# A rotary-embedding kernel: the last store in two pieces, and another row for the shared work

## Chip, cores and metric

One core of a Trainium2 chip. The metric is device time in microseconds (us) of one execution. The time is some 1.75 us above the span of the profile of the same execution, so differences can be compared between the two.

## The reference

`x` is (16, 512, 1024) float32: 16 heads of 64 in each row. Every head is rotated:

```python
x = x.reshape(batch, seq, num_heads, head_dim)
x1, x2 = (x[..., :half_dim].copy(), x[..., half_dim:].copy())
rotated = np.concatenate([x1 * cos - x2 * sin, x1 * sin + x2 * cos], axis=-1)
```

33.6 MB are read and 33.6 MB written.

## The kernel before

The work is cut into eight tiles of 128 partitions x 8 rows of 1024 values (4096 KB each), which live in five slots of one buffer `xt` and are computed in place. In each tile, row 1 goes through VectorE, TensorE and ScalarE ("own row"); one row gets its cosine product from VectorE, its sine product from GpSimd, and is added by TensorE ("shared row"); the other six rows go in pairs: GpSimd makes the sine product, VectorE the cosine product and the sum. All loads and stores of `x` are issued by SyncE on one queue.

```python
ROW_OWN, ROW_PE = 0, 3
PAIRS = ((1, 2), (4, 5), (6, 7))
...
def stores(t):
    if t == 1:
        store(0, 0, 2 * KK)      # tiles 0 and 1 together
    elif t > 1:
        store(t)                 # one tile, 8 rows, 32 KB in each partition
    if t == 2:
        load(5)
        load(6, 0, 2 * KK)
...
for t in range(NT):
    first, second, third = PAIRS
    b1 = sin_rows(t, first[0], 2)            # GpSimd
    cos_product(own_ps, t, ROW_OWN)          # VectorE
    ...                                      # own row
    p1 = pair_product(t, first[0])           # VectorE
    b3 = sin_rows(t, ROW_PE, 1)
    b2 = sin_rows(t, second[0], 2)
    pair_sum(*p1, b1)
    p2 = pair_product(t, second[0])
    cos_product(own_ps, t, ROW_PE)
    for ps, b in zip(parts(own_ps), parts(b3)):
        pe_add(ps, b)                        # TensorE
    nc.scalar.copy(out=rows(t, ROW_PE), in_=own_ps)
    b1 = sin_rows(t, third[0], 2)
    ...
    pair_sum(*p2, b2)
    p1 = pair_product(t, third[0])
    pair_sum(*p1, b1)
    stores(t)
```

Tiles and rows are counted from 0 in the code and from 1 in the text. As the first two tiles share a store, there are seven stores; "the sixth store" is that of the last tile but one and is issued near 132 us (the seventh tile's store), the seventh store is the last.

## Time and profile before

| | before |
|---|---|
| time, three runs | 163.22, 163.30, 163.31 us |
| profiled execution: time, span | 163.58, 161.8 us |
| VectorE busy | 137.8 us (85%) |
| the DMA queue of all loads and stores | 97.0% of 16 engines' span |
| last store: issued, landed | 149.9, 161.0 us |

The prediction shows the lines behind these numbers and how they are read. In the lines PE is TensorE (PEld its weight loads), DVE VectorE, ACT ScalarE, POOL GpSimd and SPq SyncE's queue of instructions; q1 is the DMA queue of the loads and stores of `x`, q14 that of instruction fetches. Two things to know ahead: a DMA is spread over 16 engines and has landed when the slowest of them has; and the DMA share and GB/s in windows count each packet whole in the window where it starts, so short windows can show more than the engines can do.

### The profile page before, as it was taken

How to read it: one execution, taken by the hardware profiler on the slowest of the kernel's cores; microseconds unless marked ns; L12 is line 12 of the kernel's file. 1: busy time of each engine (PE TensorE's matmuls, PEld its weight loads, DVE VectorE, ACT ScalarE, POOL GpSimd, SP SyncE). 2: the span in 40 equal slices, each digit the busy share in tenths (PEclk: the TensorE clock that was granted, in tenths of full speed). 3: DMA queues.
4: the chain of work that ended last, by engine and by line, in shares of the span. 5: the costliest groups of instructions: out<-in, count | busy, mean ns of one | idle time of the engine just before them, and what ended most of it. 6: DMA issues, size and time to landing. Idle time of an engine off the chain costs nothing.

```text
span 161.8 us, 432 instructions
## 1 busy us (share of the span) xinstructions
PE 64.5 (40%) x72; PEld 20.5 (13%) x72; DVE 137.8 (85%) x77; ACT 18.5 (11%) x20; POOL 126.9 (78%) x38
## 2 busy tenths in 40 slices
PE   2272671444518180818153542626090906262000
PEld 0121120202011110202020201111020202020000
DVE  1149899999999999999999999999999999999000
ACT  3010202020201010020202020202002020202000
POOL 1095999999499999999999699973999999940000
PEclk9999999995555555555855576556755585769555
DMA  5999999699699799799999999898999999996996
GB/s 171 407 410 470 405 502 518 292 486 518 275 486 535 308 470 518 340 429 397 429 464 397 478 437 502 389 405 381 437 462 397 437 462 397 446 454 275 389 389 259
DMA packets 2113, 67.25 MB, mean 416 GB/s; under 512 B 256, under 2 KB 256, under 8 KB 320
## 3 DMA queue, kind: packets, MB, share of 16 engines
q1 hardware_dynamic: 2064, 67.18, 97.0%
q10 hardware_dynamic: 48, 0.07, 0.1%
q14 instruction: 1, 0.01, 0.0%
HBM read 33.69 MB, written 33.55 MB: 416 GB/s over the span
## 4 chain that ended last, share of the span: by engine, by line
DVE 35%; DMA 33%; POOL 13%; issue 9%; PE 2%; ACT 1%; DVEq 0%; POOLq 0%; SPq 0%
DMA xt<-in_x_dram 17%; DMA out_dram<-xt 17%; DVE pd L152 15%; DVE xt L201 14%; POOL b L175 13%; DVE own_ps L152 2%; PE own_ps L186 2%; DVE xt L158 2%; ACT xt L193 1%; DVE small L119 0%; DVEq L201 0%; POOLq L175 0%; SPq L77 0%; SPq L81 0%
## 5 line engine op out<-in xcount | busy, mean ns | idle before, releaser
L175 POOL TENSOR_TENSOR b<-xt,sns 128x2048 f32<-128x2048 f32 (+1 forms) x32 | 126.2, 3987 | 15.9 <-DMA xt<-in_x_dram 15.9
L201 DVE TENSOR_TENSOR xt<-pd,b 128x2048 f32<-128x2048 f32 x24 | 54.9, 2289 | 1.6
L152 DVE TENSOR_TENSOR pd<-xt,cos_t 128x2048 f32<-128x2048 f32 x24 | 55.0, 2294 | 0.5
L186 PE MATMUL own_ps<-xt,ident 128*128 128x512 f32 x32 | 29.7, 1081 | 42.7 <-DVE xt L158 22.2
L186 PE MATMUL own_ps<-b,ident 128*128 128x512 f32 x32 | 29.7, 1085 | 33.2 <-DVE own_ps L152 30.8
L152 DVE TENSOR_TENSOR own_ps<-xt,cos_t 128x1024 f32<-128x1024 f32 x16 | 19.6, 1222 | 3.4 <-PE cos_t L122 3.0
L186 PEld LDWEIGHTS own_ps<-xt,ident 128*128 128x128 f32 x32 | 9.4, 323 | 62.4 <-issue 62.4
L186 PEld LDWEIGHTS own_ps<-b,ident 128*128 128x128 f32 x32 | 9.4, 324 | 53.5 <-issue 37.7
L193 ACT COPY xt<-own_ps 128x1024 f32<-128x1024 f32 x8 | 8.1, 1012 | 64.4 <-PE own_ps L186 64.4
L228 ACT COPY xt<-own_ps 128x1024 f32<-128x1024 f32 x8 | 8.1, 1012 | 55.1 <-PE own_ps L186 55.1
L158 DVE TENSOR_TENSOR xt<-xt,small 128x1024 f32<-128x1024 f32 x8 | 9.8, 1220 | 0.2
L123 DVE TENSOR_SCALAR sns<-small 128x256 f32<-128x256 f32 x1 | 0.4, 424 | 4.7 <-PE small L116 4.7
L116 PE MATMUL small<-sin_sb,spread 32*128 32x256 f32 x4 | 2.2, 662 | 2.8 <-DMA sin_sb<-in_sin_dram 2.8
L122 PE MATMUL cos_t<-cos_sb,spread 32*128 32x512 f32 x2 | 2.1, 1136 | 2.1 <-DMA cos_sb<-in_cos_dram 2.1
L116 PEld LDWEIGHTS small<-sin_sb,spread 32*128 32x128 f32 x4 | 1.2, 320 | 4.8 <-issue 4.8
L99 PE MATMUL own_ps<-zero 128*128 128x512 bf16 x2 | 1.0, 621 | 1.2 <-DVE zero L96 1.2
L124 ACT ACT_TABLE_LOAD x1 | 1.3, 1283 | 1.2 <-PEq L252 1.2
L96 DVE MEMSET zero<- 128x256 uint32 x1 | 0.3, 272 | 0.9 <-PEq L252 0.9
L124 ACT COPY sns<-small 128x256 f32<-128x256 f32 x1 | 0.4, 372 | 4.3 <-DVE sns L123 4.3
L127 ACT ACTIVATE sns<-small 128x256 f32<-128x256 f32 x1 | 0.4, 383 | 4.2 <-PE small L116 4.2
L122 PEld LDWEIGHTS cos_t<-cos_sb,spread 32*128 32x128 f32 x2 | 0.5, 308 | 2.8 <-DMA cos_sb<-in_cos_dram 2.8
L119 DVE COPY small<-sns 128x64 f32<-128x64 f32 x2 | 0.4, 224 | 0.4 <-ACT sns L124 0.4
(9 smaller groups left out, 1.6 us busy)
## 6 DMA issues: line engine op xcount, KB each, us to landing
out_dram<-xt SPq DMA_DIRECT2D x6, 4096.0 KB, 22.4
xt<-in_x_dram SPq DMA_DIRECT2D x3, 4096.0 KB, 21.8
xt<-in_x_dram SPq DMA_DIRECT2D x1, 2560.0 KB, 12.6
xt<-in_x_dram SPq DMA_DIRECT2D x1, 1536.0 KB, 7.2
sin_sb<-in_sin_dram ACTq DMA_DIRECT2D x1, 64.0 KB, 4.2
cos_sb<-in_cos_dram SPq DMA_DIRECT2D x1, 64.0 KB, 7.1
xt<-in_x_dram SPq DMA_DIRECT2D x2, 34.9
out_dram<-xt SPq DMA_DIRECT2D x1, 26.7
```

Source lines behind the costliest of these rows:

```text
L99: nc.tensor.matmul(out=ps, lhsT=zero[:, :P], rhs=zero, start=True, stop=True)
L116: nc.tensor.matmul(out=sin_t, lhsT=spread, rhs=part, start=True, stop=True)
L119: nc.vector.tensor_copy(out=own_t[:, u], in_=sns[:, u * KK + ROW_OWN].rearrange("p a j -> p (a j)"))
L122: nc.tensor.matmul(out=cos_t, lhsT=spread, rhs=cos_sb, start=True, stop=True)
L124: nc.scalar.copy(out=sns[:, :KK, 1, :], in_=sin_k)
L152: nc.vector.tensor_tensor(out=o, in0=i, in1=cb, op=ALU.mult)
L158: nc.vector.tensor_tensor(out=heads(r), in0=heads(r), in1=s, op=ALU.mult)
L175: nc.gpsimd.tensor_tensor(out=o, in0=i, in1=sb, op=ALU.mult)
L186: nc.tensor.matmul(out=ps, lhsT=ident, rhs=other, start=False, stop=True, skip_group_check=True)
L193: nc.scalar.copy(out=r0, in_=own_ps)
L201: nc.vector.tensor_tensor(out=r, in0=ps, in1=b, op=ALU.add)
L228: nc.scalar.copy(out=rows(t, ROW_PE), in_=own_ps)
```

## The change

Its intent is to start the last store earlier. With the shared row moved to the end, the first five rows of a tile are complete after the second of its three pair sums, so five eighths of the last tile can be stored while VectorE still works on the last pair.

```diff
-ROW_OWN, ROW_PE = 0, 3
+ROW_OWN, ROW_PE = 0, 7
-PAIRS = ((1, 2), (4, 5), (6, 7))
+PAIRS = ((1, 2), (3, 4), (5, 6))
 FIRST = 3
+LAST_OUT = 5
@@ def stores(t):
     if t == 1:
         store(0, 0, 2 * KK)
+    elif t == NT - 1:
+        store(t, 0, LAST_OUT)
+        store(t, LAST_OUT, KK)
     elif t > 1:
         store(t)
```

## The prediction

> **What bounds the kernel now.** I read the page first (busy shares, then the line of 40 slices for the DMA engines), then the chain of waits, then the last 30 us by windows, and last the time from issue to landing of each of the last stores.
>
> The page's shares and its DMA rows:
>
> ```profile
> PE 64.5 (40%) x72; PEld 20.5 (13%) x72; DVE 137.8 (85%) x77; ACT 18.5 (11%) x20; POOL 126.9 (78%) x38
> DMA  5999999699699799799999999898999999996996
> q1 hardware_dynamic: 2064, 67.18, 97.0%
> DVE 35%; DMA 33%; POOL 13%; issue 9%; PE 2%; ACT 1%; DVEq 0%; POOLq 0%; SPq 0%
> ```
>
> The fullest resource is not VectorE (85%) but the one DMA queue that carries all loads and stores (97% of 16 engines' span): 67.18 MB have to pass and they pass at a nearly constant rate. The chain of waits names VectorE most (35%), but it is the chain of the instructions that happen to end last. Whether VectorE or the queue sets the end has to be read from the last stage. Windows over it (columns: stretch and its length, then PE, PEld, DVE, ACT and POOL busy with instruction counts, granted clock, DMA share, GB/s):
>
> ```profile
> 115.00:132.50 17.50, 7.44 (x8) 2.34 (x8) 17.19 (x11) 2.02 (x2) 17.50 (x6) 0.61 1.00 431
> 132.50:148.15 15.65, 7.29 (x8) 2.34 (x8) 15.34 (x9) 2.02 (x2) 10.84 (x3) 0.67 1.01 436
> 148.15:150.20 2.05, 0.00 (x0) 0.00 (x0) 1.65 (x1) 0.00 (x0) 0.00 (x0) 0.86 0.08 32
> 150.20:161.80 11.60, 0.00 (x0) 0.00 (x0) 0.00 (x0) 0.00 (x0) 0.00 (x0) 0.50 0.84 362
> ```
>
> Until 148 us the DMA engines are full although VectorE is busy as well: the store queue has a backlog. At about 148 us it runs dry while VectorE is still at the last pair of the last tile, so for a moment VectorE does set the end. Then one whole store of 4096 KB runs by itself. The issues of the last three stores in the timeline (start, length), and under them their times from issue to landing, in the same order:
>
> ```profile
> 115.11 0.33 SPq L81 DMA_DIRECT2D out_dram<-xt  x1
> 132.49 0.33 SPq L81 DMA_DIRECT2D out_dram<-xt  x1
> 149.87 0.33 SPq L81 DMA_DIRECT2D out_dram<-xt  x1
> ...
> out_dram<-xt SPq DMA_DIRECT2D x1, 4096.0 KB, 25.7
> out_dram<-xt SPq DMA_DIRECT2D x1, 4096.0 KB, 17.9
> out_dram<-xt SPq DMA_DIRECT2D x1, 4096.0 KB, 11.1
> ```
>
> Sums: they land at 115.11 + 25.7 = 140.8, at 132.49 + 17.9 = 150.4 and at 149.87 + 11.1 = 161.0 us. The store before these (issued at 97.74, 33.4 us to landing) lands at 131.1. So inside the backlog one store lands every 9.6 us ((150.39 - 131.14) / 2 = 9.63), however early it was issued; the last one comes 10.6 us after its predecessor. The difference, 0.95 us, is all that the dry queue costs at the landing, and it is the number on which the prediction rests. After the landing 0.8 us are left to the end of the span.
>
> It is much less than the 2.05 us of nearly idle DMA in the third window. The finer windows show why:
>
> ```profile
> 148.20:148.40 0.20, 0.00 (x0) 0.00 (x0) 0.20 (x1) 0.00 (x0) 0.00 (x0) 1.00 0.38 164
> 148.80:149.00 0.20, 0.00 (x0) 0.00 (x0) 0.20 (x1) 0.00 (x0) 0.00 (x0) 1.00 0.39 164
> 149.00:150.50 1.50, 0.00 (x0) 0.00 (x0) 0.80 (x1) 0.00 (x0) 0.00 (x0) 0.71 0.00 0
> 150.50:150.80 0.30, 0.00 (x0) 0.00 (x0) 0.00 (x0) 0.00 (x0) 0.00 (x0) 0.50 3.30 1420
> ```
>
> 1420 GB/s cannot be a rate; a window counts each packet whole, where it starts. 164 GB/s x 0.2 us is 32.8 KB, one packet of one engine: so one engine starts its last packet of the sixth store at 148.2 to 148.4 and another at 148.8 to 149.0. A packet of 32,768 B takes 1.22 us (431 GB/s over 16 engines at share 1.00 is 26.9 GB/s each). The last engine is therefore busy until about 150.1, and its first packet of the last store starts after 150.5: it stood still for some 0.5 to 0.7 us, while the average engine stood still for about 1.5 us. The landing records of the trace, one for each engine, agree: the sixth store lands on 15 engines by 149.87 and on the last at 150.44, and the same 0.57 us lag is there in the stores before. A store has landed when its slowest engine has, so the slowest engine's gap counts.
>
> **What the Trainium skill says.** "DMA: Bandwidth & Descriptors", section "Queues, rings and completion order": each engine takes the descriptors of its ring in order, the engines of one transfer finish independently, and only the full count of 16 means landed. The trace agrees: even spacing of 9.6 us in the backlog, and the lagging engine. The same page, "Anatomy of one DMA": a DMA has a fixed part of about 2.0 us (fitted on the GpSimd path), and most of it is completion latency. Here the lone last store takes 11.1 us for 4.19 MB; at the 436 GB/s of the window that is 9.6 us of moving and 1.5 us fixed, of which a full queue hides the front but not the receipt at the end. "Latency and other measured facts" on that page gives about 600 ns to the first byte on the path that SyncE uses; the trace shows 149.87 to about 150.6, a bit more. The table "Measured" under "Bandwidth" gives 78% of the peak for a transfer of 1 MB alone; I do not apply that to pieces of 2.5 and 1.5 MB, as they are queued behind each other here.
>
> **The change part by part.**
>
> *The rows.* The shared row becomes the eighth and the pairs become rows 2-3, 4-5, 6-7. The built program keeps the same number and order of instructions on PE, VectorE, ScalarE and GpSimd, with the same shapes: 24 pair products of 2.29 us, 24 pair sums of 2.29 us, 32 GpSimd products, 32 + 32 matmuls. Only offsets move. For the first tile the load is split after row 3, and both orders need just rows 1-3 for the first GpSimd product and the second part for all others, so no wait moves. Cost 0. What it buys is that the first five rows of a tile are finished by the first two pair sums and the own row.
>
> *The early piece.* The timeline of the last tile:
>
> ```profile
> 138.79 1.01 ACT L193 COPY xt<-own_ps 128x1024 f32<-128x1024 f32 x1 [8.35 <-PE own_ps L186]
> 142.79 2.28 DVE L201 TENSOR_TENSOR xt<-pd,b 128x2048 f32<-128x2048 f32 x1
> 146.65 1.01 ACT L228 COPY xt<-own_ps 128x1024 f32<-128x1024 f32 x1 [6.84 <-PE own_ps L186]
> 147.50 2.29 DVE L201 TENSOR_TENSOR xt<-pd,b 128x2048 f32<-128x2048 f32 x1
> ```
>
> Row 1 is in place at 139.8, the second pair sum ends at 145.1, the shared row at 147.7, the third pair sum at 149.8. In the built program the store of five rows waits for the second pair sum and the own-row copy of the last tile and for nothing later; the store of three rows waits for the last sum and copy. So the five rows are issued at about 145.15 instead of 149.87, 4.7 us earlier. But the queue still holds the sixth store until 148 to 150. With some 0.8 us from issue to first packet the piece stands ready at 146, before even the fastest engine is free. The 4.7 us shrink to the gap.
>
> *The late piece.* It is issued at 149.87 as the whole store was, and can start at 150.6. Five eighths of 9.6 us is 6.0 us, so the slowest engine reaches the three rows at about 150.1 + 6.0 = 156, the fastest near 154.5. They are there 4 us too early, so the queue stays full to the end.
>
> *What it adds.* One more issue on SyncE (0.33 us, hidden) and packets of 20 KB and 12 KB in place of 32 KB. In the load of 20 KB rows at the start the engines moved 419 GB/s at share 0.98 (window 7.9 to 14.2), 26.7 GB/s each against 26.9: 0.8% of 9.7 us, 0.08 us. The receipt at the end stays as it is.
>
> *Sum.* Slowest engine: 150.4 + 9.63 + 0.08 = 160.1 instead of 161.0 from the rounded landings; with the records to the hundredth (150.44, and eight pairs of a 20 KB and a 12 KB packet at 0.766 and 0.460 us, 9.81) it is 160.25 instead of 160.96. So 0.7 to 0.9 us less; I take 0.8. 163.3 - 0.8 = 162.5 us, 0.5% faster.
>
> **The rivals.** (a) The full gap is won: if the average engine counted, 1.5 us or even the 2.05 us of the window, 161.8 to 161.2 us. For it speaks the empty window; against it that the lag of one engine persists from store to store. It would come true if the lag is a matter of chance in this execution. The record of an 8 KB instruction fetch of 0.32 us at 82 us, and the lag rising from 0.30 us before it to 0.57 us after, suggest part of it is regular. (b) Nothing is won: the early piece waits for the whole tile after all, or the two smaller transfers pay a second receipt in sequence. Then 163.3, or with 1 us more 164.3. The built waits speak against the first, the even spacing of queued stores against the second. (c) VectorE becomes the bound of the end: it does for the last three rows only if the queue is dry before 150.6, and it has 6 us of five rows left then. (d) A gain of 3.7 us, since just three eighths of the store remain after the last sum: 149.87 + 1.5 + 3.6 = 155. The backlog forbids it.
>
> **Range and chances.** The main doubt is which engine counts: gains from 0.3 us (slower small packets, lag a bit larger) to 1.5 us (no lag). I take 161.9 to 163.1. Two per cent is 3.3 us, more than the whole DMA gap, so within 2% is nearly sure.
>
> **What would show it.** In the profile after: an issue of 2560 KB near 145 and one of 1536 KB near 150; no empty DMA window at 148 to 150.5; the last landing near 160.2, some 9.7 to 9.8 us after that of the sixth store, with the engines now ending unevenly; unchanged groups for VectorE and GpSimd. A sixth store that lands elsewhere than at 150.4, or a last landing before 159.5 or after 160.8, would make it wrong.

## The result, and the profile after

Ratios are the mean time of one kernel's runs over that of the other's of the same rounds, so not quite the ratio of the medians that are quoted. The change was measured four times, the first time as the result proper, then as after_again, after_third and after_fourth.

| measurement | changed, median (range) | before, median (range) | ratio, 95% interval |
|---|---|---|---|
| result | 163.05 (162.51 to 163.45) | 163.32 (163.22 to 163.51) | 0.9981 (0.996 to 1.0002) |
| after_again | 162.71 (162.36 to 163.04) | 163.43 (163.20 to 163.85) | 0.9954 (0.9939 to 0.997) |
| after_third | 163.23 (162.95 to 163.60) | 163.44 (163.28 to 163.58) | 0.9988 (0.9976 to 1.000) |
| after_fourth | 163.32 (162.84 to 163.81) | 163.45 (163.24 to 164.22) | 0.9988 (0.9963 to 1.0012) |

The mean of the four ratios is 0.9978: 0.36 us of 163.4. The result's 163.05 us lies inside the predicted range, near its upper end. The mean gain is less than half of the 0.8 us forecast; only after_again comes near it (0.75 us), and in the other three measurements the interval reaches 1. In the result proper and in after_third the changed kernel also spreads more (0.94 us against 0.29, 0.65 against 0.30); in the other two the kernel before, with more runs, spreads as much (0.65 and 0.98 us).

In the profile of the changed kernel each step stands where the prediction put it. Its page, busy shares and chain of waits:

```profile
PE 64.5 (40%) x72; PEld 20.6 (13%) x72; DVE 137.8 (86%) x77; ACT 18.5 (11%) x20; POOL 126.9 (79%) x38
q1 hardware_dynamic: 2208, 67.18, 97.5%
DVE 67%; issue 16%; DMA 4%; POOL 3%; PE 2%; ACT 1%; DVEq 0%; POOLq 0%
```

No engine's work has changed. The chain of waits now says VectorE 67% and DMA 4%, which read alone would mislead: it starts at the last instruction of an engine, and the backlog in the DMA queue isn't an instruction. The windows over the end (columns as in the prediction):

```profile
132.50:148.15 15.65, 7.13 (x8) 2.35 (x8) 15.34 (x9) 2.02 (x2) 10.77 (x3) 0.68 1.01 436
148.15:150.20 2.05, 0.00 (x0) 0.00 (x0) 1.66 (x1) 0.00 (x0) 0.00 (x0) 0.79 0.84 362
150.20:161.80 11.60, 0.00 (x0) 0.00 (x0) 0.00 (x0) 0.00 (x0) 0.00 (x0) 0.50 0.71 303
```

The window that was nearly dry (share 0.08, 32 GB/s) now holds 0.84 and 362 GB/s. And the issues of the last stores in the timeline (start, length), with the time from issue to landing of each below, in the same order:

```profile
132.50 0.33 SPq L82 DMA_DIRECT2D out_dram<-xt  x1
145.16 0.33 SPq L82 DMA_DIRECT2D out_dram<-xt  x1
149.89 0.33 SPq L82 DMA_DIRECT2D out_dram<-xt  x1
...
out_dram<-xt SPq DMA_DIRECT2D x1, 4096.0 KB, 17.9
out_dram<-xt SPq DMA_DIRECT2D x1, 2560.0 KB, 11.3
out_dram<-xt SPq DMA_DIRECT2D x1, 1536.0 KB, 10.2
```

The sixth store lands at 150.4, the five rows at 145.16 + 11.3 = 156.5, the three rows at 149.89 + 10.2 = 160.1 us; before it was 161.0. The span is 161.0 against 161.8, and this execution took 162.75 us. So the pair of profiles shows the predicted 0.8 us. That is luck in part: the profile of the kernel before is of an execution of 163.58 us, slower than all six of its timed runs of the result, and that of the changed kernel is of one faster than its median. The other executions mostly did not gain as much, and what sets them apart is what the experiments had to find.

### The profile page after: what moved, and what is told of

Its sections match the earlier page's. It is cut to its first block, busy times and chain, and to the rows that moved or that the text cites. A ratio compares the mean times of both kernels' runs of the same rounds, so it can differ in the third digit from the quotient of the medians.

```text
span 161.0 us, 434 instructions
## 1 busy us (share of the span) xinstructions
PE 64.5 (40%) x72; PEld 20.6 (13%) x72; DVE 137.8 (86%) x77; ACT 18.5 (11%) x20; POOL 126.9 (79%) x38
## 4 chain that ended last, share of the span: by engine, by line
DVE 67%; issue 16%; DMA 4%; POOL 3%; PE 2%; ACT 1%; DVEq 0%; POOLq 0%
DVE pd L153 31%; DVE xt L202 25%; DVE own_ps L153 6%; DVE xt L159 5%; DMA xt<-in_x_dram 4%; POOL b L176 3%; PE own_ps L187 2%; ACT xt L194 1%; DVEq L202 0%; DVE small L120 0%; DVEq L159 0%; POOLq L176 0%
## 6 DMA issues: line engine op xcount, KB each, us to landing
out_dram<-xt SPq DMA_DIRECT2D x1, 2560.0 KB, 11.3
out_dram<-xt SPq DMA_DIRECT2D x1, 1536.0 KB, 10.2
```

## The experiments

Theory 1: the changed kernel ends when the slowest DMA engine has worked off its backlog, and how far that engine lags differs from execution to execution; the kernel before lets nearly every engine run dry and starts its last store level. Rivals: small pieces cost a varying extra; the moved rows cost something; the first measurement was chance; the sum on VectorE sets the end.

### Repeats, the rows alone, and other pieces

**after_again**: the changed kernel unaltered.

> The changed kernel, unaltered, once more. Theory 1 (lag): the changed kernel's end is the slowest DMA engine's backlog, which differs from execution to execution, while the kernel before lets every engine run dry at about 150 us and starts its last store level; so the runs spread again over 0.6 us or more (162.5 to 163.5), median near 163.0, and in the profile the span follows the landing of the sixth store on its slowest engine: last landing = that landing + 9.7 us. Theory 2 (pieces): the end costs a varying extra for two small transfers; then the distance from the sixth store's landing to the last landing varies and is over 9.9 us in a slow profile. Theory 3 (chance): the first measurement was off, now the median is 162.5 with a spread under 0.3 us.

**rows_only**: the changed kernel without the split store.

```diff
-    elif t == NT - 1:
-        store(t, 0, LAST_OUT)
-        store(t, LAST_OUT, KK)
```

> New rows and pairs, but the last tile stored whole as before. Theory 1: as the kernel before, 163.3 us within 0.15, spread under 0.35 us, last store's 16 engines landing within 0.25 us of each other. Theory 4 (the moved rows cost something that the pieces win back): 163.7 to 164.0. If the wide spread comes with the rows, it shows here.

**old_rows_six_two**: old rows and pairs, pieces of six and two rows.

```diff
-ROW_OWN, ROW_PE = 0, 7
-PAIRS = ((1, 2), (3, 4), (5, 6))
+ROW_OWN, ROW_PE = 0, 3
+PAIRS = ((1, 2), (4, 5), (6, 7))
-LAST_OUT = 5
+LAST_OUT = 6
```

> Old rows and pairs, the last tile stored in six and two rows: the six are complete when the fourth row's copy ends at about 147.7 us, so their store is issued near 147.75 and its packets are ready near 148.5, when the fastest engines have just run dry. Theory 1: as the changed kernel, 163.0 with a wide spread (0.6 us or more), because the slow engine decides and it still has work until 150; the rows are not needed. If the 4.7 us of earlier issue mattered in themselves it would lie at 163.3. Theory 2: pieces of 24 KB and 8 KB cost as much as those of 20 and 12.

**before_again**: the kernel before, unaltered.

> The kernel before, unaltered, as a null: ratio 1.000 within 0.0005, spread 0.3 us. Theory 1: its sixth store's slowest landing differs from that of the first profile by some tenths of a us, yet its last landing stays at 161.0 within 0.1 and its engines land within 0.25 us of each other. Theory 3: no difference of the sixth store's landing between profiles.

Measured on one chip: after_again 0.9954; rows_only 163.42 us, 0.9996 (0.9981 to 1.0011); old_rows_six_two 162.85 us, 0.996 (0.9946 to 0.9974); before_again 163.47 us, 0.9999 (0.9983 to 1.0014). The rows alone are worth nothing, and with the old rows a split of six and two gives what the change gives. So the moved rows were not needed. The spreads were not as clear-cut as expected: 0.68 us for after_again, 0.50 for old_rows_six_two, 0.66 and 0.53 for rows_only and before_again, whose VectorE began its work earlier or later by some tenths (their last store was issued at 149.68 and 149.75, against 149.87 before).

The profiles settle the mechanism. The sixth and the last store of after_again, issues and landings:

```profile
132.09 0.33 SPq L82 DMA_DIRECT2D out_dram<-xt  x1
149.47 0.33 SPq L82 DMA_DIRECT2D out_dram<-xt  x1
...
out_dram<-xt SPq DMA_DIRECT2D x1, 4096.0 KB, 18.6
out_dram<-xt SPq DMA_DIRECT2D x1, 1536.0 KB, 10.9
```

and of before_again:

```profile
132.37 0.33 SPq L81 DMA_DIRECT2D out_dram<-xt  x1
149.75 0.33 SPq L81 DMA_DIRECT2D out_dram<-xt  x1
...
out_dram<-xt SPq DMA_DIRECT2D x1, 4096.0 KB, 17.7
out_dram<-xt SPq DMA_DIRECT2D x1, 4096.0 KB, 11.1
```

In after_again everything on VectorE is 0.4 us earlier than in the first profile of the change, yet the sixth store takes 18.6 us in place of 17.9 and the end is at 149.47 + 10.9 = 160.4 in place of 160.1. In before_again the sixth store lands at 150.1, 0.3 us earlier than in the first profile, and the last again 11.1 us after its issue: the kernel before follows VectorE, the changed one the queue.

The landing records of each profile (one for each of the 16 engines) give the lag itself. "Lag" is the slowest engine's landing of the sixth store less the median engine's; the last columns are the time from the sixth store's landing to the last landing, and the spread of the 16 engines at the last landing.

| profile | lag | sixth to last landing | spread at the end |
|---|---|---|---|
| before | 1.17 us | 10.52 us | 0.17 us |
| before_again | 0.80 | 10.78 | 0.15 |
| rows_only | 0.66 | 10.85 | 0.15 |
| after | 1.16 | 9.72 | 1.46 |
| after_again | 1.43 | 9.72 | 1.78 |
| old_rows_six_two | 1.48 | 9.74 | 1.68 |
| after_third | 1.72 | 9.71 | 2.01 |
| after_fourth | 1.92 | 9.72 | 2.32 |

With a split store the last landing comes 9.71 to 9.74 us after the sixth, whatever the pieces, so the pieces cost nothing that varies; that rival falls. The lag is carried unchanged to the end. With a whole store the engines end level, and the lag shows in nothing but the middle column.

In this table the split kernels lag more than the others (1.16 us and up, against 1.17 and less). A rival would be that the change itself makes the lag. The lag stands already at the landing near 111 us (1.16 us in before, 1.14 in after), long before the split store is issued at 145 us, and further profiles cross over: at the sixth store the lag was 2.05 us in before_pad64 and 1.88 in before_more, with whole stores, and 0.43 in after_extra and 0.62 in one_engine, with split ones (all described below).

**after_third** and **after_fourth**: the changed kernel again, on two other chips.

> The changed kernel a third time. Theory 1 (a varying lag of the slowest engine on top of a steady 9.73 us): ratio 0.995 to 0.998, spread 0.6 us or more, and in the profile last landing = the seventh tile's slowest landing + 9.7 us. If the first measurement was the true one, the ratio is 0.998 again; if the second was, 0.9955.

> The changed kernel unaltered, on the same chip: ratio between 0.995 and 0.999 with a spread of 0.6 us or more.

Measured: 0.9988 in both (table above). The first measurement was no accident. The intervals of after_again and after_third do not overlap, so calls differ by more than noise, each on another chip. after_fourth's profile took 163.59 us; its sixth and last store:

```profile
132.40 0.33 SPq L82 DMA_DIRECT2D out_dram<-xt  x1
149.78 0.33 SPq L82 DMA_DIRECT2D out_dram<-xt  x1
...
out_dram<-xt SPq DMA_DIRECT2D x1, 4096.0 KB, 18.8
out_dram<-xt SPq DMA_DIRECT2D x1, 1536.0 KB, 11.2
```

18.8 us for the sixth store, and the last landing at 149.78 + 11.2 = 161.0: 11.2 us after its issue, where a whole store takes 11.1. An execution with such a lag has no gain left.

### More work on all engines, or on one

**after_extra**, **before_extra** and **one_engine** were meant to put known extra work into the queue by storing finished rows again. I took them from the third tile's slot:

```diff
+    if t == 5:                                   # one_engine: t == 6, one partition, 64 KB
+        place, at = run(2, 0, KK // 2)
+        at = (at[0], slice(0, 16), at[2])
+        nc.sync.dma_start(out=out_v[at], in_=place[:16])
```

> The changed kernel with 16 KB more on each of the 16 DMA engines: a repeat of 16 partitions of the third tile's store, queued behind the store of the sixth tile (about 115 us), some 0.6 us of queue time (16,384 B at 26.9 GB/s). Theory 1 (the queue is full to the end, its backlog sets the end): the seventh tile's store and the last landing both move by 0.6 us, time 0.6 us above the changed kernel's, near 163.3 to 163.4. Rival (VectorE's last sum sets the end): no change, 162.7.

> The same 16 KB on each engine in the kernel before. Theory 1: the seventh tile's store lands 0.6 us later, but the dry stretch before the last store takes it up on all engines but a late one: last landing later by 0.0 to 0.3 us, ratio to the kernel before 1.000 to 1.002. Rival (the queue sets the end here too): + 0.6 us, ratio 1.004.

> The changed kernel with 64 KB more on one DMA engine alone: a repeat of one partition of the third and fourth tiles' rows, queued behind the seventh tile's store (about 132.5 us); 2.4 us on that engine. Theory 1 (the slowest engine decides): the median engine's last landing does not move, the slowest's does, to 2.4 us behind where that engine would have been: time 1.2 us (an average engine) to 2.4 us (the lagging one itself) above the changed kernel's, 163.9 to 165.2. Rival (the work is shared or the average engine counts): + 0.15 us, below 163.0.

Measured: 167.70, 172.34 and 177.51 us, all with wrong results. The last tile is loaded into that same slot, so the repeated rows were other data and VectorE had to wait for the repeated store before it could write. Their times say nothing on the question. Mended, with slots that no later tile uses, all behind the sixth store:

```diff
     # after_more and before_more
+    if t == 6:
+        place, at = run(3, 0, KK // 2)
+        nc.sync.dma_start(out=out_v[at[0], 0:16, at[2]], in_=place[:16])
     # one_engine_more
+    if t == 6:
+        for old in (3, 4):
+            place, at = run(old)
+            nc.sync.dma_start(out=out_v[at[0], 0:1, at[2]], in_=place[:1])
```

> Mends after_extra, whose repeated rows lay in a slot that the last tile is loaded into (a wrong result and a wait of VectorE). The changed kernel with 16 KB more on each of the 16 DMA engines: 16 partitions of the fourth tile's rows, which no later tile overwrites, stored again behind the seventh tile's store (132.5 us), 0.61 us of queue time. Theory 1 (the backlog sets the end): the last landing is 0.6 us later, some 10.35 us after the seventh tile's store on the slowest engine in place of 9.73; time 163.2 to 163.5, ratio to the kernel before 0.999 to 1.000. Rival (VectorE's last sum sets the end): as the changed kernel, 162.7, ratio 0.9955.

> The same 16 KB on each engine in the kernel before. Theory 1: the stretch that is dry before the last store takes the 0.61 us up, except on an engine over 0.9 us late: last landing unchanged or up to 0.4 us later, ratio 1.000 to 1.0015. Rival (the queue's backlog sets the end here too): + 0.6 us, ratio 1.004.

> Mends one_engine in the same way. The changed kernel with 64 KB more on one DMA engine: one partition of the fourth and of the fifth tile stored again behind the seventh tile's store, 2.4 us on that engine, 0.15 us on average. Theory 1 (the slowest engine decides): 15 engines land as before near 159.5 and one 1.2 to 2.4 us after the usual last, time 163.9 to 165.2. Rival (the average counts): at most + 0.2 us, 162.9.

Measured: after_more 164.56 us, 1.0073 (1.0061 to 1.0085); before_more 164.09 us, 1.0043 (1.0023 to 1.0063); one_engine_more 164.11 us, 1.0051 (1.0034 to 1.0068).

one_engine_more took a time in theory 1's range: 2.4 us on one engine, 0.15 us on average, cost 0.76 us against the kernel before of the same call and 0.8 to 1.4 us against the changed kernel's medians (0.8 against after_fourth, on the same chip). In its landing records 14 engines land at the end within 0.83 us of each other, the usual late one 0.93 us after them and the burdened one another 0.87 us later, less than the expected 1.2 to 2.4. The slowest engine decides; that the average counts is refuted.

The 16 KB on every engine missed the numbers of theory 1, and of the rival for before_more by chance hit them. The reason was the dose and a large lag, not the mechanism: of the 16 packets of 16,384 B only 4 took 0.61 us in either run, the longest 2.86 us in after_more and 2.36 in before_more. From the sixth store to the extra one the median engine's landing moved by 1.9 us in after_more and 1.0 in before_more, the slowest landing, which is what counts, by 0.84 and 0.91. after_more's slowest engine also lagged by 2.02 us before the extra store, more than in any unaltered profile. The Trainium skill's page "SBUF — State Buffer", section "Door 1: The DMA port swizzle", would have warned me: partitions 0 to 15 reach 4 of 16 ports, for some 109 GB/s. An estimate from that page, 262,144 B at 109 GB/s, is 2.4 us; after_more's median of 1.9 us comes near it, before_more's 1.0 us does not. Read with the true dose, both kernels follow one rule. In after_more the last landing is 9.71 us after the slowest landing of the extra store; in before_more it is 9.65 us after it, since with so late an engine the last store of the kernel before no longer starts level (its engines end 1.04 us apart in place of 0.15), while its median engine keeps its usual time. The kernel before ends at whichever is later: VectorE's last sum + the lone store, or the slowest engine's backlog + a store.

### Where the lag comes from

In each profile of the kernel before and of the changed one, two packets stand out after 60 us. One of 32,768 B near 82 us takes 0.53 to 0.66 us longer than its usual 1.21; an 8 KB instruction fetch runs beside it. And near 107 to 109 us, at the end of the 8 MB load of the last two tiles, the 65,536 B packets are longer than their 2.42 us, the longest by 0.25 to 0.83 us.

The Trainium skill's page "Runtime: NRT & Kernel Launch", section "Instruction fetch mechanics", says that each sequencer fetches its next page of instructions with its own DMA queue while the current one runs, and that the cost is mostly hidden. It does not say what the fetch does to data packets on the engine that it uses. Whose fetch is it?

**fewer_matmuls** (the shared row lacks its sine part):

```diff
-    for ps, b in zip(parts(own_ps), parts(b3)):
-        pe_add(ps, b)
```

> Wrong on purpose: the changed kernel without the matmuls that add the GpSimd product of the eighth row, so TensorE's program is about half as long. Theory 1a (the 0.55 us that one engine loses near 82 us come from an instruction fetch for TensorE): the 8 KB fetch near 82 us is gone or moved, the long packet there too, the slowest engine of the seventh tile's store lands 0.3 to 0.6 us nearer to the median engine, and the time is 162.2 to 162.5 with a smaller spread. Rival (the fetch is another engine's, or the long packet has another cause): fetch and long packet stay at 82 us, time as the changed kernel, 162.7.

**loads_on_act**: the first loads of `x` and the load of cos go to ScalarE's queue, that of sin to SyncE's.

```diff
-nc.scalar.dma_start(out=sin_sb, in_=sin_v)
-load(0, 0, FIRST)
-nc.sync.dma_start(out=cos_sb, in_=cos_v)
-load(0, FIRST, KK)
+nc.sync.dma_start(out=sin_sb, in_=sin_v)
+load(0, 0, FIRST, nc.scalar)
+nc.scalar.dma_start(out=cos_sb, in_=cos_v)
+load(0, FIRST, KK, nc.scalar)
...                                   # loads of tiles 1 to 4 likewise
```

> The changed kernel, with the first five loads of x and that of cos issued from ScalarE's queue and that of sin from SyncE's, so SyncE's program is shorter. In every profile so far an 8 KB instruction fetch falls within 0.3 us of SyncE's waking for the second of the late loads (82 us), and the packet beside it is 0.53 to 0.66 us too long; it does not move with TensorE's program. Theory 1b (it is SyncE's fetch, and it makes up about half of the slowest engine's lag): it moves later or vanishes; if it vanishes, or comes when the queue no longer matters, the slowest engine lags 0.3 to 0.6 us less and the time is 162.1 to 162.4 with a narrower spread, faster than both kernels. If it only moves to a later store, the time stays at 162.7. Rival (another engine's fetch or no fetch at all): it stays at 82 us.

**dve_pad**: 32 tiny memsets ahead.

```diff
+pad = fixed.tile([P, 32], FP32)
+for i in range(32):
+    nc.vector.memset(pad[:, i : i + 1], 0.0)
```

> The changed kernel with 32 tiny memsets for VectorE at the start, where it waits for the first load. If the 8 KB fetch near 82 us is VectorE's, it moves to between 20 and 50 us, with the long packet, and the time is as the changed kernel's or 0.1 to 0.3 us less. Rival (GpSimd's or ScalarE's fetch): it stays at 82 us, same time.

**load_apart**:

```diff
-load(6, 0, 2 * KK)
+load(6)
+load(7)
```

> The changed kernel with the load of the last two tiles as two loads of 4 MB (packets of 32 KB in place of 64). Theory 1c (the second part of the lag comes from the 64 KB packets at the end of the 8 MB load): the long packets near 108 us shrink to half, the slowest engine lags 0.2 to 0.4 us less, time 0.1 to 0.4 us under the changed kernel's of the same call. Rival: the lag has nothing to do with the packet's size, same time.

**after_pad64** and **before_pad64**: as dve_pad, with 64 memsets, in the changed kernel and in the kernel before.

> The changed kernel with 64 tiny memsets for VectorE at the start (some 1 us, while it waits for the first load), so that its 8 KB fetch falls into the first 5 us instead of 82 us. Theory 1 (the fetch starts the lag, the lag eats the gain): no long packet near 82 us, the sixth store (132 us) lands 17.2 to 17.7 us after its issue in place of 17.9 to 18.7, time 162.0 to 162.5, ratio to the kernel before 0.992 to 0.995, the fastest version so far. Rival (the fetch is a bystander): long packets stay near 82 us or the lag near 108 us arises alone, time as after_fourth.

> The same memsets in the kernel before. Theory 1: it lets its queue run dry before the last store and doesn't care: 163.3 to 163.5, ratio 0.999 to 1.000. Rival (the memsets help in some other way, for instance by an earlier or later start of VectorE): ratio below 0.997.

The fetch shows as the one packet of queue 14 (queue, kind: packets, MB, share). It was found in fewer_matmuls between 81.5 and 83 us, in loads_on_act between 81 and 83, in dve_pad between 41 and 43 and in after_pad64 between 5 and 8; in this order:

```profile
q14 instruction: 1, 0.01, 1.3%
q14 instruction: 1, 0.01, 1.0%
q14 instruction: 1, 0.01, 1.0%
q14 instruction: 1, 0.01, 1.0%
```

So it is not TensorE's and not SyncE's (theories 1a and 1b fall); it moves with VectorE's instruction count, and in dve_pad the long packet moves with it, to 42.4 us and 0.61 us over, and neither dve_pad nor after_pad64 has a long packet near 82 us any more. So a fetch holds up the data packet beside it. It is not the only thing that can: before_pad64, with its fetch at 7.0 us, has three long packets at 82.1 to 82.2 us, up to 0.69 us over, and dve_pad has eleven near 50 to 52 us, 0.2 to 0.5 us over. That the fetch makes the lag is not shown:

| run | ratio to before, 95% interval | lag in its profile | longest excess near 108 us |
|---|---|---|---|
| fewer_matmuls | 0.9975 (0.9961 to 0.999) | 0.99 us | 0.23 us |
| loads_on_act | 0.9998 (0.9973 to 1.0024) | 1.10 | 0.47 |
| load_apart | 0.9985 (0.9968 to 1.0002) | 1.23 | 0.68 |
| dve_pad | 1.0019 (0.9998 to 1.0039) | 2.40 | 1.20 |
| after_pad64 | 0.9971 (0.9949 to 0.9992) | 1.47 | 0.71 |
| before_pad64 | 1.0025 (1.0007 to 1.0043) | 2.05 | 0.76 |

With the fetch at 6.7 us the lag of after_pad64 is still 1.47 us: 0.81 us at the landing near 92 us (0.62 to 1.27 in the profiles of the table above), 1.39 at that near 112 us. Its time is not clearly different from after_fourth's on the same chip (162.99 and 163.32, intervals overlap). Nor did halving the load's packets help: load_apart has excesses up to 0.68 us there. dve_pad missed its expectation: 163.80 us, where the changed kernel took 163.23 in the same call. What goes together in most profiles is the lag and the longest excess near 108 us: 0.66 to 0.80 us of lag with 0.25 to 0.32 (rows_only, before_again), 1.2 with 0.4 (before, after), 1.4 to 1.7 with about 0.6 (after_again, old_rows_six_two, after_third), 1.92 with 0.83 (after_fourth), 2.40 with 1.20 (dve_pad). fewer_matmuls (0.99 with 0.23) and load_apart (1.23 with 0.68) fall out of the order. That is a correlation. Why packets at the end of that load are long, and longest where an engine is late already, stays open; so does whether the gain depends on the chip (after_again, after_third and after_fourth ran on chips 1, 11 and 3). before_pad64 was 0.4 us slower than before, against its expectation: its sixth and last stores were issued some 0.5 us later (132.96 and 150.34 us), so VectorE was late. In after_pad64 they were only 0.15 us later than in after (132.65 and 150.03 us), so the pair with memsets (162.99 against 163.92 us) fits theory 1 but is no clean test of it.

No run beat the changed kernel clearly; old_rows_six_two equals it with fewer edits.

## Why the prediction was right or wrong

1. *The bound.* Right: a full queue until 148 us, then VectorE for a moment. The profile of the change shows the gap closed.
2. *The rows cost and bring nothing by themselves.* Right: rows_only 0.9996.
3. *The early piece gains the gap, not its 4.7 us.* Right: issued at 145.16, and the end moved 0.8 us between the two profiles, 0.36 us on average.
4. *The pieces cost 0.08 us.* Right: from the sixth to the last landing 9.71 to 9.74 us, against 9.63 + 0.08.
5. *The slowest engine counts.* Right: one_engine_more, and the level ends before against spreads of 1.5 to 2.3 us after.
6. *How late the slowest engine is.* Here it failed, in size. The term of the sum is the sixth store's slowest landing, "150.4" (150.44 us), taken from the one profile of before; the text adds that the lag "is there in the stores before". (Its 0.57 us is the distance to the second slowest engine; to the median engine the lag was 1.17 us.) That holds within one execution. Between executions it varies: in the profiles of the four measurements the lag was 1.16, 1.43, 1.72 and 1.92 us and that landing 150.37, 150.65, 150.89 and 151.21, on average 150.78. Their times follow in the same order, 162.75, 163.04, 163.26 and 163.59 us, each 12.37 to 12.39 us above the landing. So the mean of all 23 timed runs of the changed kernel, 163.08 us, stands for a landing near 150.70 (an estimate), 0.26 us later than the sum had it. The other end of the difference came from one execution as well: time less last landing is 2.62 us in before, so the mean of the 39 runs of the kernel before, 163.44 us, stands for a last landing near 160.82 in place of 160.96. Of the 0.80 us between 10.52 and 9.72 in the table that leaves 0.80 - 0.26 - 0.14 = 0.40 us; the four ratios average to 0.36. The prediction's aside that part of the lag comes with the fetch at 82 us, as it rises "from 0.30 us before it to 0.57 us after", reads two landings far apart: at 92.1 us the distance was 0.34, and only near 112 us 0.56.
7. *The range.* Rival (a) bought room for a lag by chance smaller than in the profile; larger ones were allowed only down to a gain of 0.3 us. Single executions reached 163.81 us, no gain at all. That the kernel before repeats within 0.3 us in its first runs was no sign that the lag is steady: the dry stretch had hidden it.
8. *What the Trainium skill says.* Of the first citation only the ring order stands in "Queues, rings and completion order"; that engines finish independently and that only the full 16 means landed stands in the same page's section "Why a DMA increments its semaphore by 16 and not by 1". The landing records agree with both: 16 for each of these stores, up to 2.3 us apart.

## What to carry to other kernels

Where a queue is full to the end, as here, the time is the backlog of its slowest engine, and anything that ran dry in the old version has been hiding how much that backlog varies. Before pricing the closing of a gap, take the per-engine landings of several profiles, and count the gap on the latest engine, not the mean share of a window. The first piece of the split was needed only just before the queue runs dry: issued at 147.7 us it did as well as at 145.2, so the cheapest split will do.

## What the Trainium skill lacked or had wrong

- "DMA: Bandwidth & Descriptors" says that engines finish independently, not by how much or for how long (its row on engines 7 and 15 calls them usually slower, without a figure; the traces here don't name the engine). Behind a full queue the slowest was 0.66 to 1.92 us behind the median at the sixth store in the eight profiles of the table, and in the split kernels kept that lag through the next 9.72 us.
- The same page's "Measured" table (78% of the peak for 1 MB) says nothing of queued pieces: 2.5 and 1.5 MB queued behind another store took 9.72 us together, against 9.63 us for a whole one.
- "Runtime: NRT & Kernel Launch" calls the instruction fetch mostly hidden and does not speak of data packets beside it. Beside the fetch of 8 KB one data packet was 0.53 to 0.66 us too long, and 32 more instructions on VectorE moved it from 82 to 42 us.
- No page read has long packets at the end of a load: 0.2 to 1.2 us over 2.42 us near 108 us.
- "SBUF — State Buffer" was the page to ask before the extra work was sized: storing 16 partitions of 16 KB moved the median engine's landing by 1.9 us in after_more and 1.0 in before_more, in place of 0.61.
